# One weight of a feed-forward layer split into two parts by two DMAs instead of by two engines

## Chip, cores, metric
One core of one Trainium2 chip. The metric is the device time of one launch in microseconds. The kernel before takes 1114.79 us (median of 3 runs, 1114.76 to 1116.5).

## The reference
Two transformer blocks in float32 over 512 tokens of width 1024. The first block joins block-sparse attention and a gated delta rule; the second joins a gated recurrence and sparse attention, and ends in the feed-forward layer that the change is about:

```
hn = rmsnorm(h, norm2_g[l])
h = h + jnp.square(jax.nn.relu(hn @ w_ff1[l])) @ w_ff2[l]
return rmsnorm(h, final_g)
```

`w_ff1` is 1024 x 4096 and `w_ff2` is 4096 x 1024.

## The kernel before, in words
All large products run on TensorE in the float32r format, which holds fewer bits than float32. To keep float32's accuracy each operand is split in two: a high part, the value rounded to float32r, and a low part, the value less its high part, again in float32r. A product is then three matmuls, high by high, high by low and low by high (`mm3`, line 559). ScalarE writes the high part with a copy into a float32r tile and VectorE the low part with a subtraction (`split`, line 516).

A weight comes in units of 128 x 1024 values, 512 KB. `unit` (line 544) has SP load one into a buffer `w_raw` and splits it into a buffer `w_hi` and a buffer `w_lo`. From line 1007 on there are three raw buffers (two named w_raw, and one at the end of the tile named arena) and, from line 421, three each of w_hi and w_lo. They are handed out in turn, in program order, so a w_hi buffer is written again when the matmuls on the unit three places earlier are done.

The feed-forward layer runs in four quarters of 1024 hidden columns (line 1529). Each has two parts:

- Eight units of `w_ff1` (`ff_unit`, line 1533, through `dense_T`, line 565). A unit is the stationary operand of 24 matmuls that stream the 512 tokens (tiles `ha`). ScalarE then takes the sum out of its PSUM bank with a Relu and squares it; after each second unit `quarters` splits the result into tiles `kr` and `hb`. In the first quarter the first three units run with two halves of the tokens, since the norm of the last tokens is not ready earlier.
- The product with `w_ff2`, in seven smaller products (`seventh`, line 1497). Each splits sums or differences of `w_ff2` blocks that SP loaded earlier, in two halves, into two buffers of the same w_hi and w_lo rings; 12 matmuls read each half. VectorE adds the results to the tile `x`.

So a quarter takes 8 + 14 = 22 places of the ring of three. The next quarter's first unit takes the place that the last half of the sixth of the seven products leaves; behind it only the two halves of the last product, 24 matmuls, remain of the quarter before.

The order of the instructions on each engine is not the order in which the code is written. Every call is recorded as an operation with the ones that it depends on (`record`, line 98), and a planner (`schedule`, line 198, called by `issue`, line 253) starts each operation at a planned time by prices of its own: `cost` (line 141) is how long it holds its engine, and `transfer` (line 176) how long a DMA holds the transfer engines, which start 1.9 us after the issue at the earliest. Operations are issued in order of planned start, and an engine works them off in that order: an instruction that waits holds up those behind it. All operations are issued from line 274, so the profile shows that line for each.

POOL does little: masks and memsets early, and the power -1/2 of the norms on [128 x 1] tiles (tile `sp`). All DMAs are issued by SP.

Of the kernel before, what the change touches and what calls it, by code (L numbers as in the profile page):

```python
# [26 lines left out]
F32 = mybir.dt.float32  # L27
F32R = mybir.dt.float32r
I32 = mybir.dt.int32
AF = mybir.ActivationFunctionType  # L30
OP = mybir.AluOpType
# [12 lines left out]
class Recorder:  # L44
# [53 lines left out]
    def record(self, name, method, args, kw):  # L98
        isap = lambda x: isinstance(x, bass.AP) and (not isinstance(x.tensor, bass.DRamTensorHandle)
                                                     or x.tensor.name in self.scratch)  # L100
        out = args[0]
        writes, reads = [out], list(args[1:])
        if method == "tensor_tensor_reduce":
            writes.append(args[7])
            reads = list(args[1:7])
        for k, a in kw.items():
            (writes if k == "accum_out" else reads).append(a)
        if method == "copy_predicated" or (method == "matmul" and not kw["start"]):
            reads.append(out)
        group = method == "matmul" and not (kw["start"] and kw["stop"])  # L110
        if not self.joined:
            self.ops.append(Op(name))
        i, op = len(self.ops) - 1, self.ops[-1]
        for a, w in [(a, False) for a in reads if isap(a)] + [(a, True) for a in writes if isap(a)]:
            n, p0, p1, parts, width = self.span(a)
            if a.space == PSUM:
                op.banks.add(n)
            if group and w:
                parts = [(0, width)]
            ws, rs = self.seen.setdefault(n, ([], []))  # L120
            for lo, hi in parts:
                hit = lambda e: e[0] < p1 and p0 < e[1] and e[2] < hi and lo < e[3] and e[4] != i
                for e in filter(hit, ws):
                    op.deps[e[4]] = op.deps.get(e[4], False) or not w
                if w:
                    for e in filter(hit, rs):
                        op.deps.setdefault(e[4], False)
                    for es in (ws, rs):
                        es[:] = [e for e in es if not (p0 <= e[0] and e[1] <= p1 and lo <= e[2] and e[3] <= hi)]
                (ws if w else rs).append((p0, p1, lo, hi, i))  # L130
        op.calls.append((method, args, kw))
        op.cost += self.cost(name, method, args, kw)
        if method == "activation":
            op.table = self.TABLE.get(args[2])
        if method == "matmul":
            k, m = [n for _, n in list(args[1].ap)][0], int(np.prod([n for _, n in list(args[1].ap)[1:]]))
            op.tiled = (k, m) if min(k, m) <= 64 else None
        if method == "dma_start":
            op.transfer = self.transfer(args[0], args[1])

    def cost(self, name, method, args, kw):
        size = lambda a: int(np.prod([x[1] for x in list(a.ap)[1:]])) if len(a.ap) > 1 else 1
        psum = lambda a: isinstance(a, bass.AP) and a.space == PSUM
        n = size(args[0])
        scalars = 61.0 * sum(isinstance(a, bass.AP) for a in args[2:4])
        if method == "dma_start":
            return 475.0
        if name == "tensor":
            if args[1].dtype == F32R:
                return max(n / 2.4 + 13.0, 112.0)  # L150
            if method == "transpose":
                return 110.0
            return max(n / 1.2, 107.0) + max(n, size(args[1])) / 1.2 + 4.0
        if name == "scalar":
            scaled = any(isinstance(kw.get(k), bass.AP) for k in ("scale", "bias"))
            return n / 1.2 + (51.0 if psum(args[1]) else 94.0) + 93.0 * ("accum_out" in kw) + 93.0 * scaled
        if name == "vector":
            if method == "reciprocal":
                return 6.25 * n + 69.0
            if method == "tensor_reduce":  # L160
                n = size(args[1])
            if method == "tensor_tensor_scan":
                n *= 2
            if method == "tensor_tensor":
                return n / 0.96 + 69.0
            if method == "tensor_scalar":
                return n / (0.96 if psum(args[1]) else 1.92) + 69.0 + scalars
            if method == "scalar_tensor_tensor":
                return n / 0.96 + 69.0 + 61.0 * isinstance(args[2], bass.AP)
            two = method == "tensor_copy" and not psum(args[1])  # L170
            return n / (1.92 if two else 0.96) + 67.0
        if method == "tensor_tensor":
            return n * 165.0 + 300.0 if args[3] == OP.pow else n * 2.1 + 100.0
        return n + 70.0
# [233 lines left out]
def body(ctx: ExitStack, tc: tile.TileContext, x, norm_pre_w, norm_post_w, positions, norm1_g, norm2_g, final_g,  # L408
# [4 lines left out]
    v, s, g, pe, sy = (rec.engine(n) for n in ("vector", "scalar", "gpsimd", "tensor", "sync"))  # L413
# [4 lines left out]
    def tiles(n, bufs, name, dt=F32, p=pool):  # L418
        return Ring([p.tile([128, n], dt, name=f"{name}{i}") for i in range(bufs)])

    w_raw, w_hi, w_lo = tiles(1024, 2, "w_raw"), tiles(1024, 3, "w_hi", F32R), tiles(1024, 3, "w_lo", F32R)
# [20 lines left out]
    w_in, w_out, w_in2, w_br_a, w_br_b, w_out2, w_ff1, w_ff2, cmp_w1_k, cmp_w1_v = packed  # L442
# [73 lines left out]
    def split(hi, lo, src, scale=None, e=v):  # L516
        if scale is None:
            s.activation(hi, src, AF.Copy)
            tt(e, lo, src, hi.bitcast(F32), OP.subtract)
        else:  # L520
            s.activation(hi, src, AF.Copy, scale=scale)
            v.scalar_tensor_tensor(lo, src, scale, hi.bitcast(F32), op0=OP.mult, op1=OP.subtract)
# [21 lines left out]
    def unit(w, k0, nk, *cols, place=None):  # L544
        ncol = sum(b - a for a, b in cols)
        n = nk * ncol
        raw = w_raw(128, n)
        sy.dma_start(raw, w.part(k0, nk, *cols))
        if place:
            hi, lo = place  # L550
            split(hi, lo, raw.rearrange("p (k n) -> p k n", k=hi.shape[1]))
            if nk < hi.shape[1]:
                return [a.rearrange("p (k m) n -> p k m n", k=nk) for a in place]
            return [a.rearrange("p k (m n) -> p (k m) n", n=ncol) for a in place]
        hi, lo = w_hi(128, n), w_lo(128, n)
        split(hi, lo, raw)
        return hi.rearrange("p (k n) -> p k n", k=nk), lo.rearrange("p (k n) -> p k n", k=nk)
# [7 lines left out]
    def dense_T(*units, H, parts=1):  # L565

        ws = [unit(w, 0, 8, (c0, c0 + 128)) for w, c0, _ in units]
        pss = [dn(128, T) for _ in units]
        n = T // parts
        for h in range(parts):  # L570
            ts = slice(h * n, h * n + n)
            for wu, ps in zip(ws, pss):
                for k in range(8):
                    mm3(ps[:, ts], wu, H, (ALL, k), (ALL, k, ts), k == 0, k == 7)
        for (_, _, evac), ps in zip(units, pss):
            evac(ps)

    def dense_N(w, c0, ncol, H, toks, evac, ready=(), row0=0):
        nk = 1024 // ncol
        pss = {t: dn(128, ncol) for t in toks}  # L580
        for u, k0 in enumerate(range(0, 8, nk)):
            m = min(nk, 8 - k0)
            wu = ready[u] if u < len(ready) else unit(w, row0 + k0, m, (c0, c0 + ncol))
            for t in toks:
                for k in range(m):
                    mm3(pss[t], H, wu, (ALL, k0 + k, slice(t * 128, t * 128 + 128)), (ALL, k),
                        k0 + k == 0, k0 + k == 7)
        for t in toks:
            evac(t, pss[t])
# [3 lines left out]
    def gated_unit(k0, m):  # L593

        return unit(w_in, k0, m, (1280, 1536), (4096, 4104))
# [1015 lines left out]
```

## Time and profile before

| | |
|---|---|
| median of 3 runs | 1114.79 us |
| profiled execution, its own time | 1114.45 us |
| its span, first to last instruction | 1112.7 us |
| mean granted clock of TensorE | 0.996 |
| TensorE busy | 1088.8 us, 98% |
| VectorE busy | 781.4 us, 70% |
| ScalarE busy | 582.0 us, 52% |
| POOL busy | 41.1 us, 4% |
| moved by DMA | 109.60 MB |

Busy time of TensorE is the union of its matmuls, which overlap: one of 512 columns lasts 0.39 us in the trace and the next starts 0.23 us after it. PE is the matmul and PEld the load of its stationary operand, DVE is VectorE, ACT is ScalarE. In an operation, the tile ahead of the arrow is written and those behind it are read. For a DMA, the time to landing runs from its issue to the arrival of its last bytes.

### The profile page before, as it was taken

To read this page: it belongs to the slowest core of one execution; us is meant where nothing else is said; L and a number is where in the kernel's file an instruction comes from. 1 tells how busy PE (TensorE), PEld (TensorE's weight loads), DVE (VectorE), ACT (ScalarE), POOL (GpSimd) and SP (SyncE) were. 2 spreads that over 40 slices of the span, in tenths; PEclk is the share of its full clock that TensorE was granted. 3 is DMA by queue.
4 is the path that set the end of the run, shared out by engine and by line. 5 is a ranking of instruction groups with operands and counts; after the bars stand their busy time and mean duration, and the time that the engine had idled before them with its cause. 6 is when DMAs were issued, how large, how long until landed. Compare 5 with 4: busy or idle time off the path is not lost. (4 is left out here: it accounts for less than half of the span.)

```text
span 1112.7 us, 15240 instructions
## 1 busy us (share of the span) xinstructions
PE 1088.8 (98%) x5712; PEld 901.3 (81%) x5712; DVE 781.4 (70%) x1607; ACT 582.0 (52%) x1059; POOL 41.1 (4%) x65
## 2 busy tenths in 40 slices
PE   8999999999999999999999999999999999999997
PEld 7887888787879877888777778888988888888885
DVE  7585877979666446688967654466678578488486
ACT  4655645574455534547765543345553553553564
POOL 1010101001000000000000000000000000000001
PEclk9999999999999999999999999999999999999999
DMA  5323122222542222224201163253205205205102
GB/s 214 133 87 97 50 82 82 79 61 85 177 145 87 102 84 70 67 96 142 96 20 58 44 240 112 96 167 112 102 19 187 97 19 198 105 1 208 38 1 77
DMA packets 44283, 109.60 MB, mean 99 GB/s; under 512 B 10416, under 2 KB 17968, under 8 KB 44208
## 3 DMA queue, kind: packets, MB, share of 16 engines
q1 hardware_dynamic: 44208, 108.62, 28.2%
q8 instruction: 45, 0.74, 0.3%
q14 instruction: 30, 0.25, 0.1%
HBM read 104.67 MB, written 3.93 MB: 98 GB/s over the span
## 5 line engine op out<-in xcount | busy, mean ns | idle before, releaser
L274 PE MATMUL bank<-ha,w_hi 128*128 128x512 f32 (+1 forms) x1504 | 460.7, 384 | 0.0
L274 PEld LDWEIGHTS bank<-ha,w_hi 128*128 128x128 f32 x1504 | 273.0, 189 | 46.2 <-issue 0.8
L274 PE MATMUL bank<-ha,w_lo 128*128 128x512 f32 (+1 forms) x752 | 287.0, 382 | 0.0
L274 DVE TENSOR_TENSOR w_lo<-w_raw,w_hi 128x1024 fp32r<-128x1024 f32 (+2 forms) x106 | 128.0, 1208 | 102.6 <-ACT w_hi L274 101.5
L274 ACT ACTIVATE w_hi<-w_raw 128x1024 fp32r<-128x1024 f32 (+2 forms) x106 | 110.9, 1047 | 153.8 <-PE bank L274 134.2
L274 DVE TENSOR_TENSOR w_lo<-arena,w_hi 128x1024 fp32r<-128x1024 f32 (+2 forms) x94 | 114.0, 1217 | 69.2 <-ACT w_hi L274 68.8
L274 ACT ACTIVATE w_hi<-arena 128x1024 fp32r<-128x1024 f32 (+3 forms) x102 | 102.5, 1005 | 114.9 <-PE bank L274 110.0
L274 PEld LDWEIGHTS bank<-ha,w_lo 128*128 128x128 f32 x752 | 141.8, 189 | 23.2 <-issue 0.3
L274 PE MATMUL bank<-w_hi,hb 128*128 128x512 f32 x416 | 133.6, 393 | 0.3 <-DVE x L274 0.3
L274 ACT ACTIVATE arena<-bank 128x512 f32<-128x512 f32 (+5 forms) x158 | 74.0, 484 | 60.5 <-PE bank L274 57.2
L274 PE MATMUL bank<-w_hi,ha 128*128 128x512 f32 (+3 forms) x384 | 98.1, 343 | 2.1 <-ACT w_hi L274 2.1
L274 ACT ACTIVATE arena<-arena,sp 128x384 f32<-128x384 f32 (+3 forms) x156 | 83.2, 560 | 31.8 <-DVE sp L274 28.0
L274 PE MATMUL bank<-arena 128*128 128x128 f32 (+9 forms) x672 | 96.6, 311 | 1.8 <-DVE arena L274 0.9
L274 PEld LDWEIGHTS bank<-arena 128*128 128x128 f32 (+2 forms) x672 | 76.8, 173 | 21.8 <-issue 12.3
L274 PEld LDWEIGHTS bank<-w_hi,hb 128*128 128x128 f32 x416 | 78.1, 188 | 16.8 <-DVE x L274 0.7
L274 PE MATMUL bank<-ident,arena 128*128 128x128 f32 (+1 forms) x476 | 83.4, 277 | 5.1 <-DVE arena L274 3.4
L274 PE MATMUL bank<-w_lo,hb 128*128 128x512 f32 x208 | 81.6, 392 | 0.4 <-DVE w_lo L274 0.4
L274 PEld LDWEIGHTS bank<-ident,arena 128*128 128x128 f32 (+1 forms) x476 | 58.6, 139 | 25.3 <-DVE arena L274 8.8
L274 PEld LDWEIGHTS bank<-w_hi,ha 128*128 128x128 f32 x384 | 67.0, 191 | 9.8 <-ACT w_hi L274 2.3
L274 PE MATMUL bank<-kr,hb 128*128 128x512 f32 (+3 forms) x288 | 71.3, 352 | 1.9 <-DVE sp L274 1.9
L274 DVE TENSOR_TENSOR arena<-arena 128x1024 f32<-128x1024 f32 (+9 forms) x136 | 69.3, 532 | 3.2 <-ACT arena L274 1.4
L274 POOL TENSOR_TENSOR sp<-sp,mhalf 128x1 f32<-128x1 f32 (+1 forms) x36 | 31.1, 863 | 999.6 <-DVE sp L274 994.9
(161 smaller groups left out, 1371.1 us busy)
## 6 DMA issues: line engine op xcount, KB each, us to landing
w_raw<-in_w_in_dram SPq DMA_DIRECT2D x62, 512.0 KB, 3.3
arena<-in_w_ff_dram SPq DMA_DIRECT2D x43, 512.0 KB, 4.3
w_raw<-in_w_ff_dram SPq DMA_DIRECT2D x21, 512.0 KB, 3.4
w_raw<-in_w_out_dram SPq DMA_DIRECT2D x17, 512.0 KB, 3.4
arena<-in_w_out_dram SPq DMA_DIRECT2D x9, 512.0 KB, 3.5
x<-in_x_dram SPq DMA_DIRECT2D x8, 512.0 KB, 5.6
arena<-in_w_in_dram SPq DMA_DIRECT2D x8, 512.0 KB, 3.2
arena<-blocks_x SPq DMA_DIRECT2D x8, 256.0 KB, 2.9
```

Source lines behind the costliest of these rows:

```text
L274: self.issued.append((i, getattr(getattr(self.nc, ops[i].engine), method)(*args, **kw)))
```

## The change
For units of `w_ff1` alone, POOL issues a DMA from the weight in memory straight into the float32r tile w_hi; ScalarE writes the negative of that into w_lo; and POOL issues a second DMA, which reads the same weight and adds it to w_lo. No raw buffer and no VectorE subtraction is used for these units. The planner is told of it: a DMA of POOL holds POOL for 1000 ns, and an adding DMA takes twice the transfer time and depends on what it adds to.

```
-        if method == "copy_predicated" or (method == "matmul" and not kw["start"]):
+        if method == "copy_predicated" or "accum_op" in kw or (method == "matmul" and not kw["start"]):
             reads.append(out)
...
-            op.transfer = self.transfer(args[0], args[1])
+            op.transfer = self.transfer(args[0], args[1]) * (2.0 if "accum_op" in kw else 1.0)
...
-            return 475.0
+            return 475.0 if name == "sync" else 1000.0
...
     def unit(w, k0, nk, *cols, place=None):
         ncol = sum(b - a for a, b in cols)
         n = nk * ncol
+        if w is w_ff1:
+
+            hi, lo = w_hi(128, n), w_lo(128, n)
+            g.dma_start(hi, w.part(k0, nk, *cols))
+            s.activation(lo, hi.bitcast(F32), AF.Copy, scale=-1.0)
+            g.dma_start(lo, w.part(k0, nk, *cols), accum_op=OP.add)
+            return hi.rearrange("p (k n) -> p k n", k=nk), lo.rearrange("p (k n) -> p k n", k=nk)
         raw = w_raw(128, n)
```

## Rows read from the trace of the kernel before

**Rows 1.** The page: busy us, share of the span and instructions of each engine.
```profile
span 1112.7 us, 15240 instructions
PE 1088.8 (98%) x5712; PEld 901.3 (81%) x5712; DVE 781.4 (70%) x1607; ACT 582.0 (52%) x1059; POOL 41.1 (4%) x65
```

**Rows 2.** Windows: us; busy us of PE, PEld, DVE, ACT, POOL; clock, DMA share, GB/s.
```profile
700.00:800.00 100.00, 99.26 (x521) 84.82 (x520) 60.48 (x75) 43.86 (x65) 2.22 (x4) 1.00 0.36 125
800.00:900.00 100.00, 100.00 (x443) 82.81 (x442) 70.17 (x86) 50.82 (x62) 0.00 (x0) 1.00 0.27 95
900.00:1000.00 100.00, 100.00 (x443) 82.78 (x442) 75.86 (x91) 50.31 (x60) 0.00 (x0) 1.00 0.23 85
```

**Rows 3.** Waits from 750 us to the end: us in total, times, longest.
```profile
ACT w_hi L274 <- PE bank L274: 128.8, 69, 6.3
```

**Rows 4.** Order of time, ScalarE and VectorE, two units of the second quarter.
```profile
865.10 1.06 ACT L274 ACTIVATE w_hi<-w_raw 128x1024 fp32r<-128x1024 f32 x1 [4.15 <-PE bank L274]
...
870.54 1.06 ACT L274 ACTIVATE w_hi<-w_raw 128x1024 fp32r<-128x1024 f32 x1 [3.23 <-PE bank L274]
...
871.63 1.23 DVE L274 TENSOR_TENSOR w_lo<-w_raw,w_hi 128x1024 fp32r<-128x1024 f32 x1 [3.87 <-ACT w_hi L274]
```

**Rows 5.** Order of time, ScalarE: conversions of units ahead of a lead.
```profile
772.84 1.06 ACT L274 ACTIVATE w_hi<-arena 128x1024 fp32r<-128x1024 f32 x1 [0.27 <-PE bank L274]
...
788.75 1.06 ACT L274 ACTIVATE w_hi<-w_raw 128x1024 fp32r<-128x1024 f32 x1 [6.28 <-PE bank L274]
...
854.44 1.06 ACT L274 ACTIVATE w_hi<-w_raw 128x1024 fp32r<-128x1024 f32 x1 [1.66 <-PE bank L274]
...
1017.64 1.06 ACT L274 ACTIVATE w_hi<-w_raw 128x1024 fp32r<-128x1024 f32 x1 [1.66 <-PE bank L274]
```

**Rows 6.** Order of time, TensorE: the first matmuls on these units.
```profile
776.16 0.48 PE L274 MATMUL bank<-ha,w_hi 128*128 128x256 f32 x2
...
794.38 0.63 PE L274 MATMUL bank<-ha,w_hi 128*128 128x512 f32 x2
...
859.68 0.61 PE L274 MATMUL bank<-ha,w_hi 128*128 128x512 f32 x2
...
1022.88 0.62 PE L274 MATMUL bank<-ha,w_hi 128*128 128x512 f32 x2
```

**Rows 7.** Last matmuls on w_ff1 (ns min/median/max, first and last start); window of the end.
```profile
L274 PE MATMUL bank<-ha,w_lo x280: 278/389/389, 776.5 to 1066.2; 128*128 128x512 f32 x116, 128*128 128x256 f32 x24
...
1099.00:1112.70 13.70, 5.68 (x25) 4.33 (x24) 8.40 (x14) 4.85 (x12) 1.10 (x2) 0.80 0.41 154
```

**Rows 8.** One group of VectorE from 776 to 1099 us: busy us, mean ns.
```profile
L274 DVE TENSOR_TENSOR w_lo<-w_raw,w_hi 128x1024 fp32r<-128x1024 f32 x20 | 24.4, 1222 | 25.0 <-ACT w_hi L274 24.5
```

**Rows 9.** DMA: feed-forward from 756 us; whole trace; 733 to 752 us; queue totals.
```profile
DMA to landing us min/median/max: 3.3/3.5/5.4
...
DMA to landing us min/median/max: 3.3/3.7/8.6
...
DMA to landing us min/median/max: 3.4/4.1/5.0
...
q1 hardware_dynamic: 44208, 108.62, 28.2%
```

**Rows 10.** Window at the end of the first quarter; columns as in rows 2.
```profile
851.00:857.50 6.50, 6.50 (x31) 5.37 (x30) 6.14 (x9) 2.46 (x3) 0.00 (x0) 1.00 1.00 370
```

**Rows 11.** What one issue or one small operation holds: SP, POOL over the last 400 us.
```profile
L274 SPq DMA_DIRECT2D w_raw<-in_w_ff_dram x21: 327/328/328, 756.4 to 1030.6; - x21
...
L274 POOL TENSOR_TENSOR sp<-sp,mhalf 128x1 f32<-128x1 f32 x8 | 5.3, 667 | 575.0 <-DVE sp L274 575.0
...
L274 POOL TENSOR_TENSOR sp<-sp,mhalf 128x1 f32<-128x1 f32 x3 | 2.6, 856 | 323.9 <-DVE sp L274 323.9
```

**Rows 12.** Windows at the kernel's start; columns as in rows 2.
```profile
5.00:10.00 5.00, 2.58 (x20) 1.91 (x18) 2.82 (x9) 2.05 (x7) 0.78 (x2) 1.00 1.00 401
10.00:15.00 5.00, 3.74 (x15) 3.15 (x16) 5.00 (x7) 3.61 (x6) 0.33 (x1) 0.67 1.05 387
```

## The prediction
> **What bounds the kernel now.** I read the busy table first, then the same table in stretches, then the order of time at the places that the change touches, then the transfers. [rows 1] TensorE is busy for 98% of the span, VectorE for 70%, so only 24 us of the span is idle TensorE time. The feed-forward stage is tighter still: [rows 2] from 800 to 1000 us TensorE has no idle time, and 443 matmuls of 512 columns in each 100 us make 0.226 us apiece at a granted clock of 1.00. VectorE is busy for 70 and 76% of these stretches and ScalarE for half. A matmul sets the pace there, not a conversion.
>
> The conversions do wait, and it matters for what. [rows 3] In this stage ScalarE waits 128.8 us, 69 times, for TensorE before it writes w_hi. So raw weights lie ready and the three w_hi and w_lo buffers are what is short: a conversion starts when TensorE lets a buffer go. The time from there to the first matmul that needs the buffer is what I call the lead. Between units inside a quarter, [rows 4] successive w_hi conversions are 5.44 us apart (865.10 and 870.54), which is 24 matmuls, and with three buffers the lead is two units, 10.9 us. Where a quarter begins it is shorter, since the buffers before were halves of a product of 12 matmuls: [rows 5, 6] conversion at 854.44 and first matmul of the new quarter at 859.68, and 1017.64 and 1022.88 for the last of the three quarter starts, 5.24 us each time. In the first quarter, unit 3 follows three units of which each half is short: 788.75 to 794.38, 5.63 us. At that quarter's start unit 1 is converted at 772.84 after a wait for TensorE and follows the first half of unit 0, 24 matmuls from 776.16 of 256 columns, at half of 0.226 us each, so at 778.9: lead 6.0 us. Today ScalarE and VectorE need 2.3 us after a release [rows 4] (870.54 to the end of the subtraction at 872.86), so nothing is late.
>
> **The change, part by part.** It takes 32 raw loads off SP's queue, and 32 subtractions of 1.22 us [rows 8] off VectorE, 39 us. I cost that gain at nothing: the matmuls without a gap hide it, and the stretch where TensorE does run dry, after 1099 us, lies behind the last matmul on such a weight at 1066.2 us [rows 7]. ScalarE keeps 32 passes of the same 128x1024 shape, with a scale of -1, at 1.06 us. POOL gets 64 DMAs.
>
> What it moves is the transfer. Before, the raw load went into a buffer of its own ahead of time; now the first DMA writes w_hi itself and can't be issued before TensorE's release. Behind the release stand, one after the other, the first transfer, the pass that makes its negative, and the second transfer. I call their sum the chain.
>
> The first transfer: no POOL DMA is in the trace. The nearest rows are SP's loads of the same 512 KB: [rows 9] 3.3 us at least, 3.5 median and 5.4 at most among the feed-forward loads; 4.1 median from 733 to 752 us, where eight loads follow closely. At the start of a quarter the w_ff2 loads keep them full ([rows 10] share 1.00, 370 GB/s from 851 to 857.5 us), so I take 4.1. The negation: 1.1 us, from its start to the next engine's (870.54 to 871.63 in [rows 4]). The second transfer reads the same 512 KB, adds and writes back. Its bounds are 3.3 us (adding costs nothing) and 8.6 us, the longest feed-forward load in the whole trace [rows 9]. I take 5.6: 4.1 and one more pass of 512 KB, which is 1.5 us by the queue's total ([rows 9]: 28.2% of 1112.7 us for 108.62 MB). Chain: 4.1 + 1.1 + 5.6 = 10.8 us.
>
> The Trainium skill (DMA: Bandwidth & Descriptors, Anatomy of one DMA) fits a POOL-issued transfer by 2.0 us plus its bytes at 436 GB/s, an estimate of 3.2 us for 512 KB, and no run here shows it; with that for both transfers the chain would be 7.5 us and the loss below about 10 us.
>
> Chain less lead is TensorE idle time where no other matmul is ready. None is: every matmul here reads the same ring, in the order in which its buffers were handed out, and after the release at 854.4 only the 24 matmuls already loaded are left. So: three quarter starts at 10.8 - 5.24 = 5.56 us are 16.7; unit 3 of the first quarter 10.8 - 5.63 = 5.2; its start 10.8 - 6.0 = 4.8. Together 26.7 us.
>
> Inside a quarter the lead of 10.9 just covers 10.8. But POOL works in order: the second DMA of unit n waits there for the negation, and the first DMA of unit n+1 stands behind it. From one first DMA to the next is then 4.1 + 1.1 plus the time that POOL spends on one issue. That is between 0.33 us, SP's own, and 0.86 us, POOL's small operation in this stage; I take 0.67, its mean over the last 400 us [rows 11]. The sum, 5.87, is 0.43 above the 5.44 of a unit; four units in each of four quarters make 6.9 us.
>
> The clock: [rows 12] at the kernel's start TensorE is busy for 2.6 of 5 us and in the next 5 us the granted clock is 0.67, between the levels 1.2 and 2.4 GHz; that loses 0.33 x 5 = 1.65 us. A stall of 5 us is longer than all gaps of those 5 us together, so I add it at all five places: 8.3 us; the bounds are 0 and that.
>
> POOL's other work in the last 400 us is eight powers of norms, 0.67 us each [rows 11], four of them ahead of this stage. The last of these may stand behind a waiting DMA; it feeds the last tokens of the norm, needed only in the second halves of the first units, which are late by then anyway, so nothing more. SP's loads of w_ff2 lose a neighbour in their queue. ScalarE's negation waits in order before evacuations; four accumulator banks cover a microsecond of that.
>
> Sum: 26.7 + 6.9 + 8.3 = 41.9 us on the profiled execution's 1114.45 us (span 1112.7 and 1.75 around it; 0.34 under the median of the runs shown): **1156 us**. Lower bound, both transfers at 3.3, a chain of 7.7, POOL's order harmless and no loss of clock: 3 x 2.46 + 2.07 + 1.7 = 11 us, 1125. Upper bound, 5.0 and 8.6 us, a chain of 14.7: 3 x 9.46 + 9.07 + 8.7 = 46 us of starts, (5.0 + 1.1 + 0.86 - 5.44) x 16 = 24 of order and 8.3 of clock: 78 us, 1193.
>
> **The rivals.** *Faster.* VectorE's 39 us come off something that waits for it. Its place is ahead of the stage, where 24 us of TensorE gaps are spread, and it would come by a new order that the planner finds, as the costs it plans with have changed. Of these gaps 0.74 us lie between 700 and 800 us [rows 2]; more needs better luck elsewhere. It decides if the chain stays under 5.24 us, which two transfers at their least don't allow. Time about 1111; chance 0.03.
>
> *No change.* The planner, which knows a price for each new step, keeps other matmuls for the quarter starts and the chain is hidden. Against it stands the ring: buffers are handed out in program order and it can shuffle only three. About 1115; chance 0.04.
>
> *POOL held off by VectorE.* If a POOL DMA can't be prepared while a VectorE operation of 1.22 us runs, with VectorE 70 to 76% busy [rows 2, 8], each issue may be 1.22 us longer: 2.4 us more at five places and 2.4 in each of 16 cycles, 51 us, 1207. The Trainium skill (SBUF — State Buffer, SBUF: two separate sides) tells of such a lock for VectorE's two-port modes; it says elsewhere on the page that a tensor_tensor has no such mode. The subtraction [rows 8], like VectorE's other large operations here, is a TENSOR_TENSOR, which speaks against it. Chance 0.06.
>
> *The edit doesn't do what it says.* The first DMA could copy without rounding. Then the negative cancels the weight wholly and the low part is zero; instructions and time are the same, and only the accuracy tells.
>
> **How the numbers follow.** My forecast, stalls at quarter starts with a chain between 7.7 and 14.7 us, has 0.85; a still longer chain 0.02; POOL held off 0.06; no change 0.04; faster 0.03. The range is the forecast's own, 1125 to 1193, which leaves out some 0.05 of it with the other cases. About 0.2% is what a measurement of this kernel can tell from no change; slower by more takes 0.93.
>
> **What would show it.** In the profile of the changed kernel: TensorE gaps of 3 to 9 us at five places, the ends of three quarters' products and the first quarter's start and unit 3, released by a DMA into w_lo; POOL's second DMAs waiting for ScalarE; units inside a quarter 5.5 to 6.5 us apart; VectorE's busy time down by 39 us; a dip of the granted clock after each gap. It is wrong if matmuls run on through the quarter starts, if the two transfers land in under 5 us together, or if the loss lies inside the quarters instead.

## The result, and the profile after

The changed kernel takes 1171.77 us (median of 4 runs, 1167.87 to 1175.65), the kernel before 1115.64 us beside it (1114.76 to 1116.64): a ratio of 1.0504 (95% interval [1.0485, 1.0524]), 56 us slower. The profiled execution is the longest of the four, 1175.65 us, 61.2 us over that of before; the accounts below are made against these 61.2.

The page of the changed kernel, its busy table and the two new kinds of DMA (KB each, median us to landing):

```profile
span 1173.9 us, 15258 instructions
PE 1110.0 (95%) x5712; PEld 911.1 (78%) x5712; DVE 746.4 (64%) x1575; ACT 579.5 (49%) x1059; POOL 86.8 (7%) x129
...
w_hi<-in_w_ff_dram POOLq DMA_DIRECT2D x32, 512.0 KB, 4.7
w_lo<-in_w_ff_dram POOLq DMA_DIRECT2D x32, 512.0 KB, 6.1
```

Against [rows 1], VectorE's busy time is down by 35 us, with 32 subtractions fewer. TensorE runs the same 5712 matmuls, yet is busy for 21.2 us more (1110.0 against 1088.8), and is idle for 40.0 us more (63.9 us of the span against 23.9). The two make the 61.2 us: part of the loss is waiting, and most of the other part, as shown below, is matmuls that run more slowly.

The table in stretches tells where. Up to the feed-forward stage and then four stretches of about a quarter each; columns as in [rows 2]:

```profile
0.00:778.20 778.20, 760.76 (x4187) 626.82 (x4188) 535.22 (x1304) 413.18 (x846) 39.30 (x63) 1.00 0.30 101
778.20:872.00 93.80, 85.61 (x431) 72.58 (x430) 53.87 (x70) 41.03 (x53) 10.84 (x15) 0.95 0.47 115
872.00:966.00 94.00, 85.79 (x359) 68.98 (x358) 49.72 (x63) 38.98 (x47) 11.33 (x16) 0.96 0.51 134
966.00:1058.00 92.00, 83.58 (x347) 67.41 (x346) 46.17 (x59) 37.92 (x46) 10.79 (x15) 0.94 0.49 121
1058.00:1160.00 102.00, 89.93 (x377) 72.05 (x376) 54.17 (x72) 44.25 (x58) 13.39 (x18) 0.97 0.45 113
```

Ahead of 778 us little has happened: 17.4 us of idle TensorE there, where the kernel before has 15.9 ahead of its first unit at 776.16 [rows 6]. In each quarter TensorE now stands still for 8 us and more, and its granted clock is 0.94 to 0.97, where [rows 2] have no idle time and 1.00. The waits from 740 us to the end (us in total, times, longest) name what it stands still for:

```profile
POOL w_hi L274 <- PE bank L274: 235.7, 23, 46.8
ACT w_lo L274 <- DMA w_hi<-in_w_ff_dram: 74.7, 23, 7.7
POOL w_lo L274 <- ACT w_lo L274: 69.6, 28, 8.5
...
PE bank L274 <- DMA w_lo<-in_w_ff_dram: 29.6, 13, 4.1
...
PE bank L274 <- DMA w_hi<-in_w_ff_dram: 4.4, 4, 1.5
```

Read from above, this is the chain: POOL waits for TensorE to let go of a w_hi, ScalarE for the transfer into it, POOL again for ScalarE's negative, and TensorE 13 times for the second transfer and 4 times for the first, 34.0 of the 40.0 us. ScalarE's wait of [rows 3] has become POOL's, and there is a transfer on either side of the pass behind it.

One start in order of time, the second quarter's, from the release (start, us, engine, what, and the idle time ahead with its releaser):

```profile
870.10 0.55 POOL L274 DMA_DIRECT2D w_hi<-in_w_ff_dram  x1 [46.76 <-PE bank L274]
...
874.24 1.06 ACT L274 ACTIVATE w_lo<-w_hi 128x1024 fp32r<-128x1024 f32 x1 [5.38 <-DVE arena L274]
875.60 0.87 POOL L274 DMA_DIRECT2D w_lo<-in_w_ff_dram  x1 [1.48 <-ACT w_lo L274]
...
875.82 0.61 PE L274 MATMUL bank<-ha,w_hi 128*128 128x512 f32 x2
...
877.92 0.73 PE L274 MATMUL bank<-ha,w_hi 128*128 128x512 f32 x2 [1.49 <-DMA w_hi<-in_w_ff_dram]
...
880.99 0.50 PE L274 MATMUL bank<-ha,w_lo 128*128 128x512 f32 x1 [2.33 <-DMA w_lo<-in_w_ff_dram]
```

From 870.10 to 880.99 is 10.9 us: 4.1 to ScalarE's start (VectorE's name stands beside it, but the transfer itself took 4.0 us to land), 1.4 to the second issue, 5.4 to the first matmul on w_lo. And two gaps inside that quarter, which come 20 and 33 us later:

```profile
887.95 0.56 POOL L274 DMA_DIRECT2D w_hi<-in_w_ff_dram  x1 [3.31 <-PE bank L274]
...
892.71 0.54 POOL L274 DMA_DIRECT2D w_hi<-in_w_ff_dram  x1 [4.20 <-PE bank L274]
894.03 0.87 POOL L274 DMA_DIRECT2D w_lo<-in_w_ff_dram  x1 [0.78 <-ACT w_lo L274]
...
897.85 0.86 POOL L274 DMA_DIRECT2D w_lo<-in_w_ff_dram  x1 [2.95 <-ACT w_lo L274]
898.40 0.87 POOL L274 DMA_DIRECT2D w_hi<-in_w_ff_dram  x1
900.78 0.50 PE L274 MATMUL bank<-ha,w_lo 128*128 128x512 f32 x1 [1.57 <-DMA w_lo<-in_w_ff_dram]
...
905.05 1.06 ACT L274 ACTIVATE w_lo<-w_hi 128x1024 fp32r<-128x1024 f32 x1 [5.00 <-DMA w_hi<-in_w_ff_dram]
...
906.14 0.55 POOL L274 DMA_DIRECT2D w_hi<-in_w_ff_dram  x1 [6.87 <-PE bank L274]
906.67 0.92 POOL L274 DMA_DIRECT2D w_lo<-in_w_ff_dram  x1
...
914.34 0.50 PE L274 MATMUL bank<-ha,w_lo 128*128 128x512 f32 x1 [2.39 <-DMA w_lo<-in_w_ff_dram]
```

The chain issued at 887.95 ends at 900.78, 12.8 us later, and that of 898.40 at 914.34, 15.9 us. Here the transfers of two units overlap, and three of the four transfers of the two late ones are longer than at the quarter's start. The first transfer of the second one goes out 0.55 us behind the second transfer of the unit ahead (898.40 and 897.85) and takes 6.7 us to ScalarE's start, where it was 4.1. The second transfers, one with the next unit's first transfer 1.3 us ahead of it (894.03 and 892.71), the other 0.5 us (906.67 and 906.14), take 6.8 and 7.7 us, where it was 5.4. Counted over the stage, the gaps that a DMA ends sum to 15.1 us at the four quarter starts and to 19.0 us at nine places inside the quarters.

Last, the clock around that quarter's start; columns as in [rows 2]:

```profile
872.00:876.00 4.00, 4.00 (x19) 3.31 (x18) 3.97 (x5) 1.06 (x1) 0.95 (x2) 1.00 1.05 404
876.00:880.00 4.00, 1.17 (x4) 0.31 (x3) 1.94 (x3) 1.06 (x1) 1.62 (x3) 1.00 0.95 217
880.00:884.00 4.00, 3.01 (x8) 2.41 (x9) 0.00 (x0) 1.06 (x1) 0.47 (x2) 0.67 1.07 260
884.00:888.00 4.00, 4.00 (x18) 3.24 (x17) 0.00 (x0) 0.00 (x0) 0.69 (x2) 0.90 0.75 128
```

The gap comes first, the lower clock behind it: 0.67 of 2.4 GHz, so mostly at 1.2, for the four microseconds in which TensorE works again, and 0.90 in the next. Not every gap has this behind it. The clock falls at eight places of the stage, the four starts and four of the nine places inside the quarters (819.83, 914.34, 996.40 and 1108.88 us); behind the other five it stays at 1.00. The four microseconds behind a gap of 2.39 us that ends at 914.34, and behind one of 2.75 us that ends at 1011.94:

```profile
914.30:918.30 4.00, 3.96 (x12) 3.10 (x13) 1.80 (x4) 2.28 (x3) 0.86 (x1) 0.65 0.76 150
1011.90:1015.90 4.00, 3.96 (x17) 3.30 (x18) 1.46 (x3) 2.01 (x2) 0.87 (x1) 1.00 0.71 131
```

By the distances between the starts of its matmuls TensorE loses 14.7 us at the lower clock in the eight stretches, 1.6 to 2.5 us in each. These are most of the 21.2 us of busy time for which there is no additional matmul. Another 3.8 us come from the gaps themselves: a matmul's end, which the next one otherwise overlaps, counts in full ahead of each of them. The last 2.7 us are not traced.

### The profile page after: what moved, and what is told of

Same layout as the page of the kernel before. It is cut to its first block, busy times and chain, and to the rows that moved or that the text cites. A ratio compares the mean times of both kernels' runs of the same rounds, so it can differ in the third digit from the quotient of the medians.

```text
span 1173.9 us, 15258 instructions
## 1 busy us (share of the span) xinstructions
PE 1110.0 (95%) x5712; PEld 911.1 (78%) x5712; DVE 746.4 (64%) x1575; ACT 579.5 (49%) x1059; POOL 86.8 (7%) x129
## 5 line engine op out<-in xcount | busy, mean ns | idle before, releaser
L274 PE MATMUL bank<-ha,w_hi 128*128 128x512 f32 (+1 forms) x1504 | 470.4, 392 | 4.4 <-DMA w_hi<-in_w_ff_dram 4.4
L274 PEld LDWEIGHTS bank<-ha,w_hi 128*128 128x128 f32 x1504 | 279.9, 194 | 53.6 <-DMA w_hi<-in_w_ff_dram 5.7
L274 PE MATMUL bank<-ha,w_lo 128*128 128x512 f32 (+1 forms) x752 | 292.5, 391 | 29.6 <-DMA w_lo<-in_w_ff_dram 29.6
L274 PEld LDWEIGHTS bank<-ha,w_lo 128*128 128x128 f32 x752 | 145.7, 194 | 59.2 <-DMA w_lo<-in_w_ff_dram 35.1
L274 DVE TENSOR_TENSOR w_lo<-w_raw,w_hi 128x1024 fp32r<-128x1024 f32 (+2 forms) x85 | 102.3, 1204 | 77.9 <-ACT w_hi L274 77.1
L274 ACT ACTIVATE w_hi<-w_raw 128x1024 fp32r<-128x1024 f32 (+2 forms) x85 | 88.7, 1044 | 113.3 <-PE bank L274 96.7
L274 ACT ACTIVATE w_hi<-arena 128x1024 fp32r<-128x1024 f32 (+3 forms) x91 | 90.7, 997 | 98.8 <-PE bank L274 96.1
L274 DVE TENSOR_TENSOR w_lo<-arena,w_hi 128x1024 fp32r<-128x1024 f32 (+2 forms) x83 | 100.8, 1216 | 54.0 <-ACT w_hi L274 53.9
L274 ACT ACTIVATE w_lo<-w_hi 128x1024 fp32r<-128x1024 f32 x32 | 33.9, 1060 | 110.5 <-DMA w_hi<-in_w_ff_dram 74.7
L274 DVE TENSOR_TENSOR sq<-arena 128x256 f32<-128x256 f32 x32 | 13.5, 423 | 117.6 <-ACT arena L274 116.8
L274 PE MATMUL bank<-w_lo,hb 128*128 128x512 f32 x208 | 81.6, 392 | 0.4 <-DVE w_lo L274 0.4
```

The costliest lines, as they stand in the source:

```text
L274: self.issued.append((i, getattr(getattr(self.nc, ops[i].engine), method)(*args, **kw)))
```

## The experiments

A measure that all of them share is the length of a quarter, read from the first matmul of the product that ends a quarter (the one on kr). In the kernel before, and in the changed one, at the ends of the first and the third quarter:

```profile
854.25 0.39 PE L274 MATMUL bank<-w_hi,kr 128*128 128x512 f32 x1
...
1017.44 0.39 PE L274 MATMUL bank<-w_hi,kr 128*128 128x512 f32 x1
```

```profile
869.64 0.61 PE L274 MATMUL bank<-w_hi,kr 128*128 128x512 f32 x2
...
1061.46 0.73 PE L274 MATMUL bank<-w_hi,kr 128*128 128x512 f32 x2 [1.15 <-ACT w_hi L274]
```

Two quarters lie between: 81.6 us each before, 95.9 after. Read in the same way (the ratio is to the kernel before as it was timed beside each run):

| kernel | a quarter, us | all, us | ratio |
|---|---|---|---|
| before | 81.6 | 1115.64 | 1 |
| no_dve | 81.6 | 1115.75 | 0.9997 [0.9987, 1.0006] |
| no_add | 83.6 | 1124.57 | 1.008 [1.0065, 1.0095] |
| half | 88.5 | 1140.72 | 1.0233 [1.0206, 1.0259] |
| half_fill | 85.5 | 1135.84 | 1.0179 [1.0163, 1.0194] |
| pieces | 87.5 | 1140.44 | 1.0216 [1.02, 1.0231] |
| plain2 | 90.0 | 1158.84 | 1.0386 [1.0366, 1.0406] |
| told | 96.0 | 1168.13 | 1.0472 [1.0454, 1.0489] |
| after | 95.9 | 1171.77 | 1.0504 [1.0485, 1.0524] |
| ring4 | 89.0 | 1170.88 | one run |
| pieces4 | 84.4 | 1156.61 | one run |

**Is VectorE's work worth anything?** no_dve is the kernel before without the subtraction:

```diff
-        split(hi, lo, raw)
+        if w is w_ff1:
+            s.activation(hi, raw, AF.Copy)
+        else:
+            split(hi, lo, raw)
```

> The kernel before, with the subtraction that writes the low part left out for the 32 units of w_ff1 (the low buffer keeps what it held, so their low parts are wrong). VectorE loses 39 us and nothing else changes. Theory 'chain': VectorE waits on nothing that TensorE needs here, so the time stays within 0.2% of the kernel before, 1113 to 1118 us. Rival 'VectorE is worth something': below 1111 us.

Its page:

```profile
PE 1089.4 (98%) x5712; PEld 902.4 (81%) x5712; DVE 745.6 (67%) x1575; ACT 582.1 (52%) x1059; POOL 41.1 (4%) x65
```

VectorE is relieved of 36 us [rows 1] and the time stays, within 0.13%. So there was nothing for the change to win on that side.

**One transfer behind the release, or the other, or both.** half has SP load the raw weight ahead of time, as before, and ScalarE make the high part, so that of the two DMAs the adding one alone is left behind the release:

```diff
-            g.dma_start(hi, w.part(k0, nk, *cols))
+            raw = w_raw(128, n)
+            sy.dma_start(raw, w.part(k0, nk, *cols))
+            s.activation(hi, raw, AF.Copy)
             s.activation(lo, hi.bitcast(F32), AF.Copy, scale=-1.0)
             g.dma_start(lo, w.part(k0, nk, *cols), accum_op=OP.add)
```

> Only the low part comes by DMA: the raw load by SP ahead of time as before, ScalarE writes the high part and its negative, POOL adds the weight. Behind TensorE's release stand two passes of ScalarE (2.2 us) and one adding DMA (5.4 to 6.1), 8 us in place of 10.9. Theory 'chain': against leads of 5.24 us three quarter starts lose 2.8 each, the first quarter's two places 2.4 and 2; with 1.7 us of lower clock behind each of five gaps 21 us in all, and nothing inside a quarter: 1136 us (1128 to 1145). Rival 'POOL's DMAs and their traffic cost by number': half the DMAs remain, 1143 or more, spread over the quarters.

no_add leaves the second DMA out, and its low part is only the negative:

```diff
             s.activation(lo, hi.bitcast(F32), AF.Copy, scale=-1.0)
-            g.dma_start(lo, w.part(k0, nk, *cols), accum_op=OP.add)
```

> The change without its second DMA: the low part stays the negative of the high part, so the product with it is wrong. Behind the release stand one plain DMA and one pass, 4.1 + 1.3 = 5.4 us. Theory 'chain': that is 0 to 1 us over the lead of 5.24 at the quarter starts, with a dip of the clock perhaps: 1116 to 1125 us. Rival 'cost by number of DMAs': 1143. Rival 'POOL's order': here no DMA of POOL waits for ScalarE, so it too expects nearly no loss.

plain2 keeps the second DMA and lets it overwrite the negative:

```diff
-            g.dma_start(lo, w.part(k0, nk, *cols), accum_op=OP.add)
+            g.dma_start(lo, w.part(k0, nk, *cols))
```

> The change with a second DMA that overwrites the low part instead of adding to it (so the low part is the weight itself, wrong); it waits for the same negative. It tells what the adding costs by itself. Theory 'chain': the second transfer lands like the first, 4.1 to 4.7 in place of 6.1 us, so the chain is 9.5 and the loss falls by 1.4 us at five places and nearly all of what is lost inside the quarters: 1145 to 1155 us. If the adding costs nothing: 1170 as in the changed kernel.

half and no_add came out as expected, 1140.72 and 1124.57 us; plain2 at 1158.84 is slower than it was thought to be: at the second and third quarter's start its gaps sum to 4.4 and 3.5 us, no less than the 3.8 and 3.5 of the changed kernel. Set in order, the first transfer alone costs 9 us, the second alone 25, the two in a row 43 when the second only copies and 56 when it adds. They don't sum: 9 + 25 is 34. What adds up is the time behind the release, and only its part beyond the lead costs anything. In half TensorE's only gaps over 0.5 us in the stage are at the four starts; the last three of them:

```profile
875.41 0.80 PE L274 MATMUL bank<-ha,w_lo 128*128 128x512 f32 x1 [3.33 <-DMA w_lo<-in_w_ff_dram]
...
963.83 0.80 PE L274 MATMUL bank<-ha,w_lo 128*128 128x512 f32 x1 [3.28 <-DMA w_lo<-in_w_ff_dram]
...
1052.88 0.79 PE L274 MATMUL bank<-ha,w_lo 128*128 128x512 f32 x1 [3.71 <-DMA w_lo<-in_w_ff_dram]
```

plain2 still has gaps inside the quarters, though shorter (0.63 to 0.74 us in the first three, where the changed kernel has 1.27 to 2.79). So they belong to two transfers in a row, and the adding makes them longer. How much an adding DMA asks of the 16 DMA engines follows from the POOL queue's share on the pages of no_add and of half, each of which has 32 DMAs of one kind there:

```profile
q0 software_dynamic: 4608, 16.78, 4.6%
```

```profile
q0 software_dynamic: 4608, 16.78, 8.2%
```

4.6% of 1123.5 us over 32 is 1.61 us of all engines for the first DMA, 8.2% of 1144.4 over 32 is 2.93 for an adding one. A unit needs 4.5 us of engines in the 5.44 us that a unit takes. That this is why overlapping transfers slow each other is argued, not shown.

**How much of a gap is the clock?** half_fill is half with 12 more matmuls in each of the last three quarters, ahead of the first unit, into a sum that is overwritten:

```diff
+        for _ in range(fill):
+            pe.matmul(pss[0], ws[0][0][ALL, 0], H[0][ALL, 0], start=True, stop=True)
...
-            dense_T(ff_unit(ci), H=HA)
+            dense_T(ff_unit(ci), H=HA, fill=12 if q and ci == 0 else 0)
```

> The kernel of 'half' with 12 more matmuls ahead of the first unit of the second, third and fourth quarter: they read that unit's high part, so they fall into the gap of 3.3 to 3.7 us before its low part lands, and their sums are overwritten. Theory 'the gap pulls the clock down': TensorE stays busy, the granted clock stays at 1.00 behind the gap where it was 0.50 for 4 us, and each of three quarters is 2 to 2.6 us shorter: 1133 to 1136 us against 1140.7. Rival 'the clock dips for another reason, or nothing is lost by it': 1140 or more, up to 1149 if the 36 matmuls only add.

As expected: 36 matmuls more, 4.9 us less. Those gaps are shorter now, and the four microseconds behind each of them are at 1.00 (the last row, columns as in [rows 2], is behind the first):

```profile
873.04 0.50 PE L274 MATMUL bank<-ha,w_lo 128*128 128x512 f32 x1 [0.73 <-DMA w_lo<-in_w_ff_dram]
...
958.68 0.50 PE L274 MATMUL bank<-ha,w_lo 128*128 128x512 f32 x1 [1.01 <-DMA w_lo<-in_w_ff_dram]
...
1044.62 0.50 PE L274 MATMUL bank<-ha,w_lo 128*128 128x512 f32 x1 [1.31 <-DMA w_lo<-in_w_ff_dram]
...
876.00:880.00 4.00, 4.00 (x20) 3.30 (x19) 0.00 (x0) 1.85 (x3) 0.00 (x0) 1.00 0.89 216
```

Together they are 7.3 us shorter (10.3 to 3.05), which doesn't quite pay for the 36 matmuls at 0.226 us, 8.1 us. Without the clock half_fill would be 0.9 us slower than half; it is 4.9 faster, so 5.8 us, 1.9 a gap, was matmuls at a lower clock behind the gaps. (By the quarters of the two profiled executions, 88.5 and 85.5, it is 3.3 a gap; that execution of half took 1146.11 us, above its median.) Behind the gap that ends at 875.41 in half the granted clock is:

```profile
876.00:880.00 4.00, 4.00 (x11) 3.13 (x10) 0.00 (x0) 0.00 (x0) 0.00 (x0) 0.50 1.07 274
880.00:884.00 4.00, 4.00 (x17) 3.24 (x16) 0.00 (x0) 0.78 (x1) 0.00 (x0) 0.84 0.27 55
```

0.50 is the lower level throughout: 11 matmuls in 4 us where 443 in 100 us [rows 2] make 18.

**The lead, or POOL's order and crowded DMA engines?** ring4 gives w_hi and w_lo a fourth buffer each, for one raw buffer fewer and a smaller arena; two of the rings in the arena (not the three of the expectation) are cut to one, so the first block's values are overwritten while still needed.

```diff
-ARENA = 17280
+ARENA = 16448
...
-    w_raw, w_hi, w_lo = tiles(1024, 2, "w_raw"), tiles(1024, 3, "w_hi", F32R), tiles(1024, 3, "w_lo", F32R)
+    w_raw, w_hi, w_lo = tiles(1024, 1, "w_raw"), tiles(1024, 4, "w_hi", F32R), tiles(1024, 4, "w_lo", F32R)
...
-    y_ring = [ar.ring(T, 2), ar.ring(T), ar.ring(T)]
+    y_ring = [ar.ring(T), ar.ring(T), ar.ring(T)]
...
-    r_khT, r_vb = ar.ring(T, 2), ar.ring(T, 2)
+    r_khT, r_vb = ar.ring(T), ar.ring(T, 2)
```

> The changed kernel with four buffers each for high and low parts (one raw buffer fewer, and three rings of the first block shortened to make room, so the whole time says little; the length of a quarter does: 81.6 us before, 94 to 96 in the changed kernel). A fourth buffer makes the lead at a quarter's start 8 us and inside it 16 us. Theory 'chain against lead': the start still loses 3 us and a dip of the clock, nothing inside: 86 to 88 us. Rival 'POOL's order and crowded transfer engines set the pace inside a quarter': only the start gets better: 90 us or more.

Its total doesn't help, since the smaller arena costs time ahead of the stage: the first kr row of the table's kind stands at 887.26 us, 17.6 us later than in the changed kernel. Its quarters do: 89.0 us against 95.9, between what the theory and its rival expected, and all TensorE gaps over 0.5 us in the second and third quarter are at the starts; the second's:

```profile
894.63 0.70 PE L274 MATMUL bank<-ha,w_hi 128*128 128x512 f32 x2 [0.86 <-DMA w_hi<-in_w_ff_dram]
899.07 0.80 PE L274 MATMUL bank<-ha,w_lo 128*128 128x512 f32 x1 [3.74 <-DMA w_lo<-in_w_ff_dram]
```

The same 64 DMAs stand in line on POOL, and the same bytes go through the same engines; yet the gaps inside the quarters are gone. This alone would not rule POOL out, since with only eight units in a row a longer lead could also hide a small loss in each. But the first DMAs there wait for TensorE, not behind others on POOL:

```profile
911.81 0.55 POOL L274 DMA_DIRECT2D w_hi<-in_w_ff_dram  x1 [4.43 <-PE bank L274]
...
916.79 0.55 POOL L274 DMA_DIRECT2D w_hi<-in_w_ff_dram  x1 [0.98 <-PE bank L274]
```

Four of them in a row (906.82 to 922.23) go out 5.0 to 5.4 us apart, so POOL and the DMA engines keep pace with units of 5.44 us. So inside the quarters too it is the chain against the lead. At the starts the fourth pair doesn't bring the 3 us that were expected of it: the gaps sum to 4.6 and 4.4 us at the second and third quarter's, where the changed kernel has 3.8 and 3.5. The second transfer is longer in ring4 (median 7.3 us to landing in the stage, against 6.1).

pieces keeps three pairs and shortens the chain instead, by column halves:

```diff
+            far = w.part(k0, nk, *cols)
+            for i in range(2):
+                c = slice(i * n // 2, (i + 1) * n // 2)
+                g.dma_start(hi[:, c], far[:, c])
+                s.activation(lo[:, c], hi[:, c].bitcast(F32), AF.Copy, scale=-1.0)
+                g.dma_start(lo[:, c], far[:, c], accum_op=OP.add)
```

> The changed kernel with both DMAs and the negation cut in halves by columns, so that the adding DMA of the first half runs while the second half is still on its way, and the first matmuls wait for the first half alone. Theory 'chain against lead': the chain to the first matmul falls from 10.9 to about 8 us, so the loss falls by 2 to 3 us at five places: 1145 to 1163 us. Rival 'POOL's 128 issues or the transfer engines set the pace': 1170 or more.

1140.44 us, better than any theory had it: 31 us less than the changed kernel, with twice the issues and POOL busy for 132.0 us, not 86.8. TensorE's waits for these DMAs are 13, where they were 17, and above all shorter:

```profile
PE bank L274 <- DMA w_hi<-in_w_ff_dram: 6.8, 6, 2.1
...
PE bank L274 <- DMA w_lo<-in_w_ff_dram: 6.0, 7, 1.6
```

12.8 us where it was 34.0. With fewer and shorter gaps the granted clock falls at two places of the stage (867 and 1045 us), where it fell at eight; the expectation had left that out. The rival, that issues are what costs, falls. Among the runs that keep all three steps behind the release and three buffers this is the fastest, and it is still 24 us slower than the kernel before.

pieces4 joins the two, the halves and ring4's buffers.

> The change with a fourth pair of w_hi and w_lo buffers (as in ring4, which overwrites values of the first block that are still needed) and with both DMAs and the negation in column halves (as in pieces). Theory, chain less lead plus the clock behind each gap: the halves cut the chain to the first matmuls by 2 to 3 us and the fourth pair adds 2.7 us of lead at a quarter's start and 5.4 inside it, so the gaps of pieces (1.6 us and less) close; quarters of 82 to 84 us, 1115 to 1128 us in all. Rival, two POOL transfers per unit are too much for the DMA engines or for POOL's order whatever the lead: quarters stay at the 86 to 89 us of pieces and of ring4, 1138 us or more.

The total missed its range, 1156.61 us, because the expectation left out what ring4 had already shown, the price of the smaller arena: the first quarter's kr row comes 28 us later than in pieces (886.63 and 858.76). The quarters, 84.4 us between these two rows, are 0.4 over the theory's range and well under the rival's 86 to 89:

```profile
886.63 0.39 PE L274 MATMUL bank<-w_hi,kr 128*128 128x512 f32 x1
...
1055.49 0.39 PE L274 MATMUL bank<-w_hi,kr 128*128 128x512 f32 x1
```

With a shorter chain and a longer lead most of the stage's loss is gone, 2.8 us a quarter out of 14.3, though every unit still makes all its transfers from POOL.

**Is it the planner's prices?** told lets the planner that orders the instructions believe that a POOL transfer starts 1 us later:

```diff
-                wire = done = max(wire, t + 1900.0) + op.transfer
+                wire = done = max(wire, t + (1900.0 if n == "sync" else 2900.0)) + op.transfer
```

> The changed kernel, with the planner told that a DMA of POOL starts its transfer 1 us later than one of SP. Theory 'chain against lead': the order is a little different but the chain is the same, 1163 to 1175 us. Rival 'the loss inside the quarters comes from an order planned by wrong prices': below 1160.

1168.13 us, 0.3% under the changed kernel, with quarters of 96.0 us where they were 95.9: another price gives another order, but hardly another time.

None of these beats the kernel before. There TensorE has no gap in this stage, and no_dve shows that the work taken away was worth nothing, so no form of this change tried here had anything to win.

## Why the prediction was right, and where it was not

**Direction and cause.** 1156 us was forecast, in a range of 1125 to 1193, by a chain of two transfers and a pass that is longer than the lead; 1171.77 was measured, by that cause. The forecast loss was 41.9 us on the profiled execution, where 61.2 are found.

**The chain: right at three starts of four.** Forecast 4.1 + 1.1 + 5.6 = 10.8 us; at the second quarter's start 4.1 + 1.4 + 5.4 = 10.9, at the first and third 11.5 and 10.6, at the fourth 14.5. One more pass of the bytes for the adding was near enough: the adding DMA holds the engines for 1.3 us more than the first one, where one more pass was put at 1.5. The Trainium skill (DMA: Bandwidth & Descriptors, Anatomy of one DMA) gives 2.0 us plus the bytes at 436 GB/s, 3.2 us as an estimate for 512 KB; the trace doesn't agree, with 3.7 us at least and 4.7 in the median for the first DMA and 5.2 and 6.1 for the adding one, and the measurement decides.

**The starts: too dear.** 21.5 us were forecast at the four quarter starts (16.7 + 4.8), 15.1 us of gaps are there. The step said of other matmuls that are ready "None is", and so charged the whole chain to the first matmul on the unit. But four matmuls need no second transfer: two on this unit's w_hi begin at 875.82, and two on the next unit's at 877.92, 3 us ahead of the first on w_lo. They fill 1.3 us, and the lead was 5.7 us (870.10 to 875.82), not 5.24; so 3.8 us of the 5.56 are left.

**Inside the quarters: the step that failed.** It priced POOL's order, "5.87, is 0.43 above the 5.44 of a unit", at 6.9 us, with 5.2 more for the first quarter's unit 3, and had "the lead of 10.9 just covers 10.8" beside it. Found are 19.0 us, at nine places, only 1.3 of them at that unit 3. That margin of 0.1 us was no margin: it took the chain of a quarter's first unit for the chain inside, where two units' transfers overlap and it is 12.8 and 15.9 us at the two gaps shown. And POOL's order is not what the loss goes by: POOL stands idle until TensorE lets a buffer go ahead of the first DMAs of 887.95, 892.71 and 906.14, as it does in ring4. (That of 898.40 stands directly behind a second DMA, but TensorE lets its buffer go at most 0.3 us earlier. In the fourth quarter those of 1067.94 and 1093.52 stand so too; what that cost was not separated.) Of the sign "TensorE gaps of 3 to 9 us at five places" little came: of the 17 gaps that these DMAs end, two reach 3 us. By the prediction's own sentence "if the loss lies inside the quarters instead" it was more than half wrong on the place: 19.0 of 34.0 us. That the sum of the two steps, 33.6 us, meets the 34.0 is luck: one error makes up for the other.

**The clock: the term mis-sized.** 1.65 us a place was forecast, at five places, 8.3 us. Found are 14.7 us at eight places, 1.8 us each. The price was near and the count was not: four gaps inside the quarters bring a dip of their own, and five do not. half_fill shows that the dip comes from the gap: where most of the gap is filled, the clock stays up. Of the 19.3 us that were missing in the sum, this term makes 6.4 and the gaps 0.4. Another 6.5 are the rest of the 21.2 us of busy time, and 6.0 are idle time that no POOL DMA ended, among it 2.0 us at 1061.46 and 1063.00, where the next product's own conversions are late; the prediction had no term for either.

**VectorE's 39 us at nothing: right**, shown by no_dve. **POOL held off by VectorE: not seen.** The first DMA's issue takes 0.55 us in the median, 0.89 at most, and the measured chain at the starts has no place for 1.22 us more at each issue. **Whether the first DMA rounds** no run here shows; the times would be the same.

## What to carry to other kernels

A load that goes ahead into a buffer of its own cost nothing here behind the release of the buffer that the matmuls read; the same load aimed at that buffer stands behind it with its whole latency. Before a step is moved from an idle engine to a DMA, set the time from release to first use beside the sum of everything that will then stand between, taken with two units in flight, and count every place at which it is short. On TensorE a gap can be paid for twice, once as idle time and once as the clock behind it; here 8 of 13 places were. Where such a chain can't be avoided, cutting it in pieces can pay although it doubles the issues: 31 of 56 us here.

## What the runs showed of the hardware

A DMA from POOL that adds holds the 16 DMA engines for 2.93 us for 512 KB into fp32r, one that only writes for 1.61 us, and POOL itself for 0.87 and 0.55 us an issue. In plain2, where the second DMA only copies, the same second transfer lands in 4.4 us in the median, not 6.1. And a gap of 3.3 us on TensorE was followed by 4 us at the lower clock throughout and another 4 at 0.84, while one of 2.75 us was followed by none.
